# A two-layer trunk on one core: memory input, root columns, chunk steps and the last sums placed differently

## Chip, core and metric

The kernel runs on one core of one Trainium2 chip. The metric is the device time of one execution in microseconds; the median of three runs of the kernel before is 1064.99 us (1062.97 to 1065.62).

## What is computed

With the depth given, one layer of the trunk is run on x of 1024 tokens by 1024 features. RMS norm of x; a combined projection gives queries and keys q, k (4 heads of 96), values v (4 heads of 192), an output gate o, an input and a forget gate for each head, and queries for the memory. q and k pass a causal convolution of four taps and a SiLU. The mLSTM runs over chunks of 128 tokens with a running maximum:

```
s   = (q k^T) * w                      # w = exp(log weights - running maximum), causal
num = s v + a * (q C);  den = sum(s) + a * (q n)
h   = num / max(|den|, exp(-m))
C   = decay * C + (k*u)^T v ;  n = decay * n + sum(k*u)
```

Beside it, four heads attend to 256 memory vectors, whose keys and values are a projection of the RMS norm of mem. Both results, side by side, go through the output projection and are added to x. Then come RMS norm, a squared-ReLU MLP of width 4096, another addition, and a last RMS norm. All is float32.

## The kernel before

Tokens are worked on in two halves h of 512, with features on the 128 partitions. Each float32 product is made of three products of rounded parts (`mm3`, lines 110 to 112): high by high, high by low, low by high. So each weight tile goes through `load_w`: a load on SP's queue into one of 4 raw buffers, a rounding copy on ACT (L91) and a subtraction on POOL (L103) into one of 5 buffers. Activations are split likewise by `split` and `split_scaled` (L119 on ACT, L120 on DVE).

`run(dense, side, every)` weaves two generators: after every `every`-th step of the dense products it traces one step of the side work, and one function out of `later` (the convolutions of a group of blocks, appended when its products are done). With `finish` the rest of the side work is traced behind the dense one. What is traced sets priorities: a scheduler orders each engine's queue by a simulated timeline, taking what is ready and traced first, and places buffers of a ring as they come free. `tc.issue_after(i)` puts what a block traces on i's engine behind i; `tc.keep_in_program_order` does so among the instructions given to it. On the chip each engine and each DMA queue then takes its list in order.

The stages that the change touches, in order:

- `project_qk(0)`: 8 steps over the feature blocks k, with 6 product banks of PSUM; x is loaded through the ring `xr` of two buffers, split, squared. In step k = 6 the root over features is made (`rms`, L133 on, and `rms_cols`, L183, which moves the roots into columns by four small copies on DVE, L188). Behind it six scalings (L285), and in `later` six convolutions (L243 to L256).
- `project_v(0)`: 16 steps in two halves of 8, 4 banks each.
- `memory_load` reads mem in four loads through the ring `xr`; each is split into two blocks of `xm` and squared into `accm`. `xm` is the second buffer of the ring `qk`, whose first is written by L285. `memory_zeros` fills parts of the key and value matrices.
- `project_qmem(0)`, `memory_kv`: queries, keys and values of the memory; `rms` and `rms_cols` of accm stand behind the first key product of the second block. The root columns are read by the scaling of the values (L438). Beside them runs `gates(0)`, whose scan over columns (L471 on DVE) feeds a transposition on PE (gp, L476).
- `project_qk(1)`, then `project_v(1)`, 16 steps each, with the four chunks of the first half beside them: each `mlstm_chunk` has two yields, scores and keys (a), sums and state (b), and what follows the second yield, the output (c), runs on into the next chunk's a: nine pieces. In b, PE writes two heads' state sums into each of two banks (c, L548); DVE reads a head's sum (L552) before PE writes the other head's into the same bank.
- `last_chunk`: the last eighth of the second MLP product, output blocks b, first half 0 (512 tokens), then half 1 in two ranges of 256 (tok1, tok2). Every output block is added into x (L1241, or L1329 for the last two), squared on ACT, and the squares are added up on DVE (L1247, put off by `lag` until `flush`). `root_first` adds them over the partitions by products with ones (ssq_o, L159), and makes a root; `root_last` ends it (L172 to L176); `write` scales and stores.

Of the kernel before, what the change touches and what calls it, by code (L numbers as in the profile page):

```python
# [14 lines left out]
P = 128  # L15
# [3 lines left out]
HT = 512  # L19
# [16 lines left out]
def trunk_kernel(ctx, tc, a, out):  # L36
# [174 lines left out]
    def seq(*gens):  # L211
        for g in gens:
            yield from g


    att = ExitStack()
    mem = att.enter_context(tc.tile_pool(name="mem", bufs=1))
# [124 lines left out]
                    f()  # L342
            yield

    def query_weight(h, b, u):
        return load_w(a["w_qm"][b, u], 512, f"qm{h}{b}{u}")

    def query_ahead():

        st["qm_w", 0, 0, 0] = query_weight(0, 0, 0)  # L350
        yield

    def project_qmem(h):
        qm = mem.tile([P, 2, 2, HT], F32R, tag="qm", name=f"qm{h}")
        st["qm", h] = qm
        for b in range(2):
            p = ps(f"qm{h}{b}")
            for u in range(2):
                w = st.pop(("qm_w", h, b, u), None) or query_weight(h, b, u)
                for kk in range(4):  # L360
                    k = 4 * u + kk
                    c = slice(kk * P, (kk + 1) * P)
                    mm3(p, w[:, 0, c], w[:, 1, c], xa[:, 0, k], xa[:, 1, k], k == 0, k == KB - 1)
                if u == 0:
                    yield
            t = at.tile([P, HT], F32, tag="cacc", name=f"qmt{h}{b}", bufs=2)
            V.tensor_tensor(t, p, st["rbc", h], ALU.mult)
            split(qm[:, b, 0], qm[:, b, 1], t)
            yield
# [29 lines left out]
    def memory_kv():  # L399
        xm, acc = st["xm"]  # L400
        pk = []
        for b in range(2):
            p = ps(f"mk{b}")
            pk.append(p)
            for u in range(2):
                w = load_w(a["w_mk"][b, u], 512, f"mk{b}{u}")
                for kk in range(4):
                    k = 4 * u + kk
                    cc = slice(kk * P, (kk + 1) * P)
                    mm3(p[:, :NMEM], w[:, 0, cc], w[:, 1, cc], xm[:, k, 0], xm[:, k, 1], k == 0, k == KB - 1)  # L410
                if (b, u) == (1, 0):
                    parts = wpool.tile([P, 2, 512], F32R, tag="w", name="sums_m", bufs=5)
                    rbc, c = rms(acc, NMEM, "m", [parts[:, i] for i in range(2)])
                    rk = rms_cols(c, NMEM, "m")
                yield
        for b, p in enumerate(pk):
            t = at.tile([P, HT], F32, tag="cacc", name=f"mkt{b}", bufs=2)
            V.tensor_tensor(t[:, :NMEM], p[:, :NMEM], rbc[:, :NMEM], ALU.mult)
            for e in range(2):
                rows = slice(64 * e, 64 * e + 64)  # L420
                own = slice(NMEM * e, NMEM * e + NMEM)
                A.activation(kbd[rows, b, 0, own], t[rows, :NMEM], AF.Copy)
                V.tensor_tensor(kbd[rows, b, 1, own], t[rows, :NMEM], kbd[rows, b, 0, own], ALU.subtract)
        pv = [ps(f"mv{t}") for t in range(2)]
        for u in range(4):
            w = load_w(a["w_mv"][u], 512, f"mv{u}")
# [6 lines left out]
                        k == 0, k == KB - 1)  # L433
            if u < 3:
                yield
        for t in range(2):
            s = at.tile([P, HT], F32, tag="cacc", name=f"mvt{t}", bufs=2)
            V.tensor_scalar(s[:, :NMEM], pv[t][:, :NMEM], rk[:, t:t + 1], None, ALU.mult)  # L438
            s = s[:, :NMEM].rearrange("p (b e d) -> p b e d", b=2, e=2)
            for b in range(2):  # L440
                split(vmem[:, t, 0, b, 0::2], vmem[:, t, 1, b, 0::2], s[:, b])
# [236 lines left out]

    chunks = lambda h: seq(*(mlstm_chunk(h, t) for t in range(TPH)))

    run(project_qk(0), seq(wait(3), memory_zeros()))
    nc.sync.dma_start(gbias, a["gbias"].partition_broadcast(P))
    nc.sync.dma_start(whn, a["whn"].partition_broadcast(P))
    run(project_v(0), seq(memory_load(), wait(4), query_ahead()))
    run(seq(project_qmem(0), memory_kv()), seq(wait(3), gates(0)))
    run(project_o(0), tiles(0))
    run(seq(project_qk(1), project_v(1)), chunks(0), every=2)
    rest = seq(gates(1), tiles(1), chunks(1))
    run(seq(project_qmem(1), project_o(1, lambda k: transpose_y(0, k))), rest, finish=False)
    run(project_out(0, lambda k: transpose_y(1, k)), rest)  # L690
# [527 lines left out]
    def last_chunk():  # L1218
# [90 lines left out]
        tok2 = slice(HQ, HT)  # L1309
        acc2 = cm.tile([P, HT], F32, tag="acc", name="oacc2")  # L1310
        late = []
        for b in range(0, KB - 2, 2):
            p = ps(f"f2{b}2")
            for e in range(2):
                products(1, b + e, tok2, p, e * HQ)
            if b == 4:
                part = root_first([(ones, acc1[:, :HQ])], HQ, "o1")
            add(x1[1][:, b:b + 2, tok2], p.rearrange("p (e t) -> p e t", e=2), acc2, b == 0, f"2{b}")
            scale(1, [b, b + 1], tok2)
            if b == 0:  # L1320
                keep(V.tensor_tensor(acc1[:, :HQ], acc1[:, :HQ], acc1[:, HQ:], ALU.add))
        r1 = root_last(part, HQ, "o1")
        write(1, 0, tok1, r1, G)
        flush()
        for b in (KB - 2, KB - 1):
            p = ps(f"f2{b}2")
            products(1, b, tok2, p, 0)
            x = x1[1][:, b, tok2]
            keep(V.tensor_tensor(x, x, p[:, :HQ], ALU.add))  # L1329
            late.append(fp.tile([P, HT], F32, tag="sum", name=f"sq_o2{b}", bufs=3)[:, :HQ])  # L1330
            A.activation(late[-1], x, AF.Square)
        write(1, 2, tok1, r1, V)
        part = root_first([(ones, s) for s in [acc2[:, :HQ], acc2[:, HQ:], *late]], HQ, "o2")
        scale(1, [KB - 2, KB - 1], tok2)
# [79 lines left out]
```

## Time and profile before

| | |
|---|---|
| median of three runs | 1064.99 us (1062.97 to 1065.62) |
| profiled execution | 1062.4 us, of which the span of the trace is 1060.7 |
| PE busy | 1035.6 us, 98% of the span |
| DVE, POOL, ACT busy | 696.7 us (66%), 592.7 (56%), 545.5 (51%) |
| mean granted clock of PE | 0.993 |

The span runs from the first to the last instruction of one execution. Shares of busy time are averages over stages with different limits. PE is the matrix engine (PEld its weight loads), DVE the vector engine, ACT the scalar engine, POOL the general one, SP the engine whose queue issues the loads and stores. A releaser is inferred from semaphores.

### The profile page before, as it was taken

To read this page: it belongs to the slowest core of one execution; us is meant where nothing else is said; L and a number is where in the kernel's file an instruction comes from. 1 tells how busy PE (TensorE), PEld (TensorE's weight loads), DVE (VectorE), ACT (ScalarE), POOL (GpSimd) and SP (SyncE) were. 2 spreads that over 40 slices of the span, in tenths; PEclk is the share of its full clock that TensorE was granted. 3 is DMA by queue.
4 is the path that set the end of the run, shared out by engine and by line. 5 is a ranking of instruction groups with operands and counts; after the bars stand their busy time and mean duration, and the time that the engine had idled before them with its cause. 6 is when DMAs were issued, how large, how long until landed. Compare 5 with 4: busy or idle time off the path is not lost.

```text
span 1060.7 us, 14584 instructions
## 1 busy us (share of the span) xinstructions
PE 1035.6 (98%) x5018; PEld 887.1 (84%) x5018; DVE 696.7 (66%) x1122; ACT 545.5 (51%) x1050; POOL 592.7 (56%) x448
## 2 busy tenths in 40 slices
PE   9989999999999999999999999999999999999996
PEld 7988998899998888877888888887778888888885
DVE  6596885952766457996534433434899888878557
ACT  7464773344754354465665565555454433443273
POOL 6755435554424475004755566565568787776455
PEclk9999999999999999999999999999999999999999
DMA  7443333232324466326555453437775545544124
GB/s 223 115 126 109 115 122 87 69 93 89 99 60 120 151 190 196 100 65 215 198 186 184 155 189 134 172 120 239 258 212 174 158 142 167 152 137 139 54 78 158
DMA packets 81802, 152.46 MB, mean 144 GB/s; under 512 B 8096, under 2 KB 26560, under 8 KB 80192
## 3 DMA queue, kind: packets, MB, share of 16 engines
q1 hardware_dynamic: 81584, 151.51, 45.5%
q8 instruction: 39, 0.64, 0.3%
q14 instruction: 35, 0.29, 0.1%
q10 hardware_dynamic: 144, 0.03, 0.0%
HBM read 114.52 MB, written 36.19 MB: 142 GB/s over the span
## 4 chain that ended last, share of the span: by engine, by line
PE 73%; DVE 8%; DMA 6%; issue 5%; POOL 5%; ACT 3%; SPq 0%; DVEq 0%; POOLq 0%; ACTq 0%
PE fX L110 5%; PE fX L112 5%; PE fX L111 5%; DMA hr<-hd 4%; PE gX L112 3%; PE gX L111 3%; PE gX L110 3%; PE wo L110 3%; PE wo L112 3%; PE wo L111 3%; PE fZ L111 2%; PE fZ L110 2%; PE fZ L112 2%; PE o L110 2%; PE o L111 2%
## 5 line engine op out<-in xcount | busy, mean ns | idle before, releaser
L116 DVE TENSOR_TENSOR hb<-hr,hb 128x1024 fp32r<-128x1024 f32 x53 | 88.5, 1670 | 9.1 <-ACT hb L115 8.9
L1142 DVE TENSOR_TENSOR xo<-xo,gX 128x512 f32<-128x512 f32 x112 | 74.3, 682 | 26.9 <-PE gX L112 22.8
L111 PE MATMUL gX<-hb,w_b 128*128 128x512 f32 x224 | 87.3, 390 | 1.6 <-DVE hb L116 1.6
L110 PE MATMUL gX<-hb,w_b 128*128 128x512 f32 x224 | 86.4, 391 | 0.5 <-ACT hb L115 0.4
L112 PE MATMUL gX<-hb,w_b 128*128 128x512 f32 x224 | 85.5, 391 | 1.0 <-POOL w_b L797 1.0
L91 ACT ACTIVATE w_b<-S_b 128x512 fp32r<-128x512 f32 x56 | 34.9, 628 | 75.4 <-PE gX L112 33.5
L115 ACT ACTIVATE hb<-hr 128x1024 fp32r<-128x1024 f32 x53 | 55.8, 1053 | 32.4 <-DMA hr<-hd 32.0
L103 POOL TENSOR_TENSOR w_wo<-r_wo,w_wo 128x512 fp32r<-128x512 f32 x32 | 45.4, 1425 | 48.4 <-ACT w_wo L91 47.0
L797 POOL TENSOR_TENSOR w_b<-r_b,w_b 128x512 fp32r<-128x512 f32 x42 | 68.5, 1644 | 5.9 <-ACT w_b L91 5.9
L748 POOL TENSOR_TENSOR S_b<-r_b,r_b 128x512 f32<-128x512 f32 x28 | 44.9, 1605 | 32.7 <-DVE w_b L797 27.1
L797 POOL TENSOR_TENSOR w_a<-r_a,w_a 128x512 fp32r<-128x512 f32 x30 | 39.4, 1312 | 38.3 <-ACT w_a L88 37.5
L103 POOL TENSOR_TENSOR w_v<-r_v,w_v 128x388 fp32r<-128x388 f32 x32 | 39.5, 1245 | 31.9 <-ACT w_v L91 31.8
L103 POOL TENSOR_TENSOR w_o<-r_o,w_o 128x384 fp32r<-128x384 f32 x32 | 33.5, 1054 | 41.2 <-ACT w_o L91 41.2
L103 POOL TENSOR_TENSOR w_qk<-r_qk,w_qk 128x384 fp32r<-128x384 f32 x32 | 38.5, 1218 | 26.8 <-ACT w_qk L91 26.8
L110 PE MATMUL fX<-xa,w_a 128*128 128x512 f32 x128 | 50.1, 391 | 1.5 <-ACT hq L1004 1.2
L111 PEld LDWEIGHTS gX<-hb,w_b 128*128 128x128 f32 x224 | 42.1, 188 | 10.8 <-DVE hb L116 2.2
L110 PE MATMUL wo<-xa,w_wo 128*128 128x512 f32 x128 | 51.0, 400 | 0.0
L112 PEld LDWEIGHTS gX<-hb,w_b 128*128 128x128 f32 x224 | 42.1, 188 | 10.5 <-POOL w_b L797 1.8
L110 PEld LDWEIGHTS gX<-hb,w_b 128*128 128x128 f32 x224 | 41.9, 188 | 10.6 <-DVE xo L1142 1.0
L111 PE MATMUL wo<-xa,w_wo 128*128 128x512 f32 x128 | 50.1, 391 | 0.0
L112 PE MATMUL wo<-xa,w_wo 128*128 128x512 f32 x128 | 50.0, 390 | 0.0
L111 PE MATMUL fX<-xa,w_a 128*128 128x512 f32 x128 | 49.9, 389 | 0.0
(396 smaller groups left out, 3450.2 us busy)
## 6 DMA issues: line engine op xcount, KB each, us to landing
hr<-hd SPq DMA_DIRECT2D x53, 512.0 KB, 3.7
r_b<-w_ff SPq DMA_DIRECT2D x56, 256.0 KB, 3.0
hd<-hq SPq DMA_DIRECT2D x54, 256.0 KB, 2.0
hd<-hq SPq DMA_DIRECT2D x12, 1024.0 KB, 4.1
r_a<-w_ff SPq DMA_DIRECT2D x36, 256.0 KB, 2.7
r_wo<-w_out SPq DMA_DIRECT2D x32, 256.0 KB, 2.7
r_a<-w_ff SPq DMA_DIRECT2D x13, 512.0 KB, 4.6
r_v<-w_v SPq DMA_DIRECT2D x32, 194.0 KB, 2.4
```

Of the source, the lines that this page charges most:

```text
L91: st["first_part"] = A.activation(dst, src, AF.Copy).ins
L103: i = engine.tensor_tensor(w[:, 1, :n], raw[:, :n], w[:, 0, :n], ALU.subtract)
L110: keep(T.matmul(out, lhsT=lh, rhs=rh, start=start, stop=False, skip_group_check=goes_on))
L111: keep(T.matmul(out, lhsT=lh, rhs=rl, start=False, stop=False, skip_group_check=goes_on))
L112: keep(T.matmul(out, lhsT=ll, rhs=rh, start=False, stop=stop, skip_group_check=goes_on))
L115: A.activation(hi, src, AF.Copy)
L116: V.tensor_tensor(lo, src, hi, ALU.subtract)
L748: i = (on or (V if both is not None and sums_on_v and key != "S4" else G)).tensor_tensor(t, x, y, op)
L797: low = engine.tensor_tensor(w[:, 1], src, w[:, 0], ALU.subtract)
L1142: V.tensor_tensor(x, x, banks[e], ALU.add)
```

## The change

It does five things. `memory_load` is traced from the sixth step of `project_qk(0)` on, in turns with `memory_zeros` (a new helper `turns`), and what is left of both behind that projection; before, it ran from the first step of `project_v(0)`, and `memory_zeros` from the fourth step of `project_qk(0)`. The first query weight of the memory, which was loaded and split four steps after the memory input (`query_ahead`), is loaded in its own stage. `rms_cols` of the memory stands behind the values' products, and `issue_after` the last subtraction of the keys. The chunks of the first half take a step at every third step of `project_qk(1)`, and what is left at every second of `project_v(1)`. In the last range, the sum over partitions of the range before stands between the two products of b = 4, the squares of b = 4 are no longer added to those before but given to the last sum as two terms of their own, and the put-off addition of b = 2 follows b = 4's addition into x.

```diff
+    def turns(*gens):
+        gens = list(gens)
+        while gens:
+            for g in list(gens):
+                if next(g, gens) is gens:
+                    gens.remove(g)
+                else:
+                    yield
...
-    def query_ahead():
-
-        st["qm_w", 0, 0, 0] = query_weight(0, 0, 0)
-        yield
...
-                w = st.pop(("qm_w", h, b, u), None) or query_weight(h, b, u)
+                w = load_w(a["w_qm"][b, u], 512, f"qm{h}{b}{u}")
...
-                    rbc, c = rms(acc, NMEM, "m", [parts[:, i] for i in range(2)])
-                    rk = rms_cols(c, NMEM, "m")
+                    rbc, cols = rms(acc, NMEM, "m", [parts[:, i] for i in range(2)])
...
-                V.tensor_tensor(kbd[rows, b, 1, own], t[rows, :NMEM], kbd[rows, b, 0, own], ALU.subtract)
+                keys_made = V.tensor_tensor(kbd[rows, b, 1, own], t[rows, :NMEM], kbd[rows, b, 0, own],
+                                            ALU.subtract).ins
...
+        with tc.issue_after(keys_made):
+            rk = rms_cols(cols, NMEM, "m")
...
-    run(project_qk(0), seq(wait(3), memory_zeros()))
+    run(project_qk(0), seq(wait(5), turns(memory_load(), memory_zeros())))
...
-    run(project_v(0), seq(memory_load(), wait(4), query_ahead()))
+    run(project_v(0))
...
-    run(seq(project_qk(1), project_v(1)), chunks(0), every=2)
+    steps = chunks(0)
+    run(project_qk(1), steps, every=3, finish=False)
+    run(project_v(1), steps, every=2)
...
+        def add_last(x, p, nm):
+            keep(V.tensor_tensor(x, x, p, ALU.add))
+            sq = fp.tile([P, HT], F32, tag="sum", name=f"sq_o2{nm}", bufs=3)
+            flat = sq[:, :HQ] if len(x.shape) == 2 else sq.rearrange("p (e t) -> p e t", e=2)
+            A.activation(flat, x, AF.Square)
+            late.extend([sq[:, :HQ]] if len(x.shape) == 2 else [sq[:, :HQ], sq[:, HQ:]])
+
         for b in range(0, KB - 2, 2):
             p = ps(f"f2{b}2")
-            for e in range(2):
-                products(1, b + e, tok2, p, e * HQ)
+            products(1, b, tok2, p, 0)
             if b == 4:
                 part = root_first([(ones, acc1[:, :HQ])], HQ, "o1")
-            add(x1[1][:, b:b + 2, tok2], p.rearrange("p (e t) -> p e t", e=2), acc2, b == 0, f"2{b}")
+            products(1, b + 1, tok2, p, HQ)
+            x, halves = x1[1][:, b:b + 2, tok2], p.rearrange("p (e t) -> p e t", e=2)
+            if b < 4:
+                add(x, halves, acc2, b == 0, f"2{b}")
+            else:
+                add_last(x, halves, b)
+                flush()
...
-        flush()
         for b in (KB - 2, KB - 1):
...
-            x = x1[1][:, b, tok2]
-            keep(V.tensor_tensor(x, x, p[:, :HQ], ALU.add))
-            late.append(fp.tile([P, HT], F32, tag="sum", name=f"sq_o2{b}", bufs=3)[:, :HQ])
-            A.activation(late[-1], x, AF.Square)
+            add_last(x1[1][:, b, tok2], p[:, :HQ], b)
```

## Rows read from the trace of the kernel before

**Rows 1.** Waits of PE: line waited for, us in total, times, longest.
```profile
PE v L111 <- POOL w_v L103: 2.5, 2, 1.7
PE c L548 <- DVE C L552: 1.9, 1, 1.9
...
PE gp L476 <- DVE gaT L471: 1.7, 1, 1.7
PE gX L111 <- DVE hb L116: 1.6, 1, 1.6
...
PE v L110 <- ACT w_v L91: 1.1, 1, 1.1
```
**Rows 2.** Windows: length, each engine's busy us (instructions), PEclk, DMA share, GB/s.
```profile
40.00:60.00 20.00, 20.00 (x115) 20.00 (x114) 19.50 (x33) 10.64 (x23) 10.19 (x8) 1.00 0.39 104
...
76.00:80.00 4.00, 4.00 (x14) 3.65 (x13) 2.39 (x6) 3.90 (x8) 3.41 (x3) 0.57 0.73 194
103.00:107.00 4.00, 4.00 (x18) 4.00 (x19) 3.50 (x10) 2.95 (x8) 0.88 (x1) 0.57 0.56 157
206.00:210.00 4.00, 3.99 (x16) 3.92 (x17) 4.00 (x9) 1.75 (x3) 2.92 (x3) 0.58 0.01 2
...
735.00:741.00 6.00, 4.43 (x20) 3.26 (x19) 5.09 (x4) 4.24 (x7) 5.96 (x5) 1.00 0.57 206
```
**Rows 3.** Timeline of PE at the end: start, us, instruction, idle before and releaser.
```profile
1050.29 1.10 PE L159 MATMUL ssq_o<-oacc,ones 128*128 128x256 f32 x4 [1.85 <-DVE oacc L1247]
1051.23 1.03 PE L159 MATMUL ssq_o<-sq_o,ones 128*128 128x256 f32 x4
```
**Rows 4.** Tile xm: count, ns min/median/max, first and last start, form.
```profile
L120 DVE SCALAR_TENSOR_TENSOR xm<-xm,small,xm x8: 473/476/477, 44.9 to 71.3; 128x256 fp32r<-128x256 f32 x8
```
**Rows 5.** Tile accm, the same columns.
```profile
L129 DVE TENSOR_TENSOR accm<-accm,sq_m x3: 677/678/1777, 64.3 to 75.7; 128x512 f32<-128x512 f32 x3
L125 ACT ACTIVATE accm<-xm x1: 617/617/617, 25.6 to 25.6; 128x512 f32<-128x512 f32 x1
```
**Rows 6.** Timeline of ACT late in project_v(0).
```profile
63.52 0.62 ACT L128 ACTIVATE sq_m<-xm 128x512 f32<-128x512 f32 x1
64.04 0.62 ACT L91 ACTIVATE w_qm<-r_qm 128x512 fp32r<-128x512 f32 x1
...
65.70 0.51 ACT L91 ACTIVATE w_v<-r_v 128x388 fp32r<-128x388 f32 x1
...
72.04 0.61 ACT L128 ACTIVATE sq_m<-xm 128x512 f32<-128x512 f32 x1
72.56 0.51 ACT L91 ACTIVATE w_v<-r_v 128x388 fp32r<-128x388 f32 x1
```
**Rows 7.** Timeline of DVE at the end of project_qk(0).
```profile
34.97 0.72 DVE L144 STREAM_TRANSPOSE rt_x<-ssq_x 128x512 f32<-128x512 f32 x1 [9.56 <-PE ssq_x L142]
```
**Rows 8.** Timeline of DVE, memory stage and project_qk(1): root columns, scan.
```profile
98.76 3.49 DVE L188 COPY rk_m<-rc_m 32x2 f32<-32x2 f32 x4
102.28 0.41 DVE L471 TENSOR_TENSOR_SCAN gaT<-gaT 16x128 f32<-16x128 f32 x1
...
181.31 0.64 DVE L188 COPY rk_x<-rc_x 32x4 f32<-32x4 f32 x4
```
**Rows 9.** Timeline of PE in project_qk(1): half of the state sums.
```profile
199.28 0.82 PE L548 MATMUL c<-v,uk 128*96 128x193 f32 x4
```
**Rows 10.** Timeline of DVE in project_qk(1): the first read of them.
```profile
204.27 0.41 DVE L552 SCALAR_TENSOR_TENSOR C<-C,gdec,c 96x193 f32<-96x193 f32 x1
```
**Rows 11.** Timeline of DVE at the end.
```profile
1045.61 0.45 DVE L161 STREAM_TRANSPOSE rt_o<-ssq_o 128x256 f32<-128x256 f32 x1 [1.27 <-PE ssq_o L159]
...
1049.49 0.65 DVE L1247 TENSOR_TENSOR oacc<-oacc,sq_o 128x512 f32<-128x512 f32 x1
1050.06 0.74 DVE L1329 TENSOR_TENSOR xo<-xo,f 128x256 f32<-128x256 f32 x2
```
**Rows 12.** Timeline of ACT at the end.
```profile
1050.51 0.75 ACT L1331 ACTIVATE sq_o<-xo 128x256 f32<-128x256 f32 x2 [0.89 <-DVE xo L1329]
```

More of the change, by code (lines that the diff above doesn't have):

```diff
@@ L343, in project_o @@
             yield
-    def query_weight(h, b, u):
-        return load_w(a["w_qm"][b, u], 512, f"qm{h}{b}{u}")
-    def query_ahead():
-        st["qm_w", 0, 0, 0] = query_weight(0, 0, 0)
-        yield
     def project_qmem(h):
```

## The prediction

> **What bounds the kernel now.** Read the waits of TensorE first, longest at the top [rows 1]. One engine, PE, is nearly always busy, so the time is the matmuls plus the few gaps in them, and the question for each edit is which gap it can close. Three places carry almost all of it, two of them in one wait each. Place A is project_v(0): three waits on converted w_v weights (2.5 in two, 1.1 in one). Place B is the memory stage: 1.7 us for the scan of the gate columns (gp <- gaT). Place C is the first mLSTM half beside project_qk(1): 1.9 us, c <- C. Then come the stretches [rows 2]: the columns to read are PE busy and PEclk. Behind each of A, B and C there are 4 us in which PE is busy throughout, but at a mean granted clock of 0.57 or 0.58, that is partly at 1.2 instead of 2.4 GHz; 4 x 0.43 = 1.7 us are lost in each. So a gap costs more than its length: A 3.6 + 1.7 = 5.3, B 1.7 + 1.7 = 3.4, C 1.9 + 1.7 = 3.6. The fourth place is the tail, where PE is out of products at 1050.29 - 1.85 = 1048.44 [rows 3] and what follows is a chain over DVE, ACT, PE and DMA. All other waits of PE are shorter.
>
> Trace against rule: the gap of 1.6 us on gX [rows 1] was followed by no slow stretch, its window stands at 1.00 [rows 2], while 1.7 us at B was. The Trainium skill, "TensorE: Matmul & The Clock Gate", section "What's actually happening", says that the stretch over which the gate judges runs freely and doesn't start with the kernel; by it the same gap may cost the clock in one execution and not in the next. By that the 1.7 us that go with the gaps of A and of B below are gained in some executions only, and a gain of 10.6 us could shrink to 7.2.
>
> **Part 1, memory input into project_qk(0); the query weight no longer ahead (place A).** Moved are 4 loads on SP's queue, 8 scalings on ACT, 8 on DVE (476 ns each, 3.8 us), 4 squares on ACT, 3 additions on DVE (0.68 + 0.68 + 1.78 = 3.1 us) [rows 4, 5]; that is 6.9 us of DVE. The four zero steps go between them and later. Nothing is added; the one query weight (load, copy, subtraction) goes back to its own stage.
> Why A waits is read on ACT, which takes its work in order [rows 6]: the copy of a w_v weight at 65.70 stands behind a memory square (63.52) and the query weight's copy (64.04), each 0.52 us from its start to the next; the copy at 72.56 stands behind a square at 72.04. Taking them away brings the first copy forward by 1.0 us, more than half of the waits' mean (3.6 / 3 = 1.2), and the second by 0.5 plus whatever DVE gains, for the convolution's activations on ACT wait for DVE. On SP the w_v loads stop queuing behind the memory loads, on POOL behind the query weight's subtraction. Bounds: if the work finds DVE's idle 9.6 us before 34.97 [rows 7], all of A goes (5.3). If it stays where DVE is busy for 19.50 of 20 us [rows 2], only ACT's queue is shortened: 1.0 + 0.5 to be gained. The other end is a loss and is the third rival. I take 5.3: the first scalings ran at 44.9 [rows 4], early in that stretch, and the waits of A come at the end of the stage, when 3 of 4 memory steps would be long done. Its cover is that nothing needs the memory input before memory_kv; with that cover gone the mk products would wait instead.
> The page "SBUF — State Buffer" of the Trainium skill, section "Who interferes with whom", speaks against this part: a DVE operation with two SBUF inputs and a POOL operation that reads SBUF exclude each other. In the trace the last of the three additions took 1.78 instead of 0.68 us [rows 5]. By the rule the eight scalings, brought beside the w_qk and w_v subtractions of POOL, could each be stretched likewise by 1.1 us, 8.8 us in all, which is another way into the third rival; by the row of the eight, at 473 to 477 ns [rows 4], they cost 3.8.
>
> **Part 2, root columns behind the keys (place B).** Four copies on DVE, 3.49 us from 98.76 [rows 8], stand ahead of the scan at 102.28, for which PE waits. They now stand behind the last key subtraction. The scan can start at about 98.8, 3.5 us earlier, which is more than the 1.7 us wait: the wait and its slow stretch go, 3.4. What is late next is the keys, and they too come earlier. Behind the copies on DVE are now only the two scalings of the memory values, whose result is first used two tiles later in project_o(0); at worst they are as late as today. The price of the copies is 3.49 at most and 0.64 at least, which is what four such copies took at 181.31 [rows 8]. Bounds of the part: 0, if the key operations slip ahead of the scan, to 3.4; I take 3.4, for the scan's input is there first.
>
> **Part 3, chunk steps spread wider (place C).** Nothing is added. In project_qk(1) a step now comes after every third k instead of every second, and the last four of nine fall into project_v(1). In C PE had written one half of the state sums at 199.28; DVE read them only at 204.27 [rows 9, 10], since the convolutions of the first three blocks stood in its queue, and the second half shares the bank. With the new spacing there is less chunk work before the convolutions, so the lag of DVE should shrink; but step 3 (of 0 to 8) now falls behind product step 11, where step 5 fell, just behind the same convolutions, and the steps of chunks 2 and 3 run beside the convolutions of the second group and with four product banks open instead of three. Bounds: +3.6 (C goes), -3.6 (C stays or moves, and a second like it comes in project_v(1)). The nearest row is C's own, so neither end: I take +1.0.
>
> **Part 4, the tail.** The sum for the second range is now between the two blocks of b = 4, so DVE's transposition (1045.61) comes earlier, and the addition of squares at 1049.49 goes: 0.57 us to the next start [rows 11]. The diff has one such addition less in the loop, not three; in its place stand two more terms in the last sum. That sum took 8 instructions from 1050.29 to 1052.26, 0.246 each [rows 3]; now there are 12, 2.95 us. The last two additions into x (1050.06) can't both come before the products end, at 1048.44: they move forward by at most 1.6, and the last square with them, from 1051.26 [rows 12] to 1049.6. The first ten instructions need older terms and can start at 1048.44; so the sum ends at 1048.44 + 2.95 = 1051.4, 0.9 earlier. Bounds: 1.0 later (twelve from the old start) to 2.1 earlier (only the last two, 0.5, behind the last square). I take 0.9. What follows, root, scaling and output, is unchanged.
>
> **Sum.** 5.3 + 3.4 + 1.0 + 0.9 = 10.6 us. It is made against the profiled execution, 1062.4 us (span 1060.7); that lies 2.6 under the median of the runs, 1064.99, which is what I subtract from: 1054.4 us.
>
> **The rivals.**
> First, A stays in the main: the memory scalings can't use the idle stretch. For it: the first load had landed when ACT squared it at 25.6, yet DVE first scaled at 44.9, after 9.6 idle us [rows 4, 5, 7]; something other than data held them, as the first write to the other buffer of their ring. Then 1.5 + 3.4 + 1.0 + 0.9 = 6.8 us, 1058.2. Against it: ACT's queue is shorter in any case.
> Second, DVE becomes the bound in project_v(1): C stays or moves and a second such gap comes. 5.3 + 3.4 + 0.9 - 3.6 = 6.0 us, 1059.0. For it: DVE's lag of 5 us at C. With the first rival too, 2.2 us: 1062.8, no change.
> Third, slower: the 6.9 us of memory work on DVE, now ahead in the order, push the convolutions of project_qk(0) back by as much; ACT waits in order for them, and w_v copies stand behind. A's wait grows from 3.6 to 10.5 us and takes a second slow stretch, 1.7. Against B's 3.4 and the tail's 0.9 that is 6.9 + 1.7 - 4.3 = 4.3 us more, 1069.3. It decides the sign once the push is over 4.3 us, or 2.6 with the second slow stretch. For it: DVE's 19.50 of 20 us; against: most of that work already ran in the same stretch.
> Fourth, the planner that orders each queue places the moved steps where they were: B and the tail alone, 4.3 us, 1060.7.
>
> **Chances.** Forecast 0.46; first 0.16; second 0.15; first and second together 0.08; third 0.09; fourth 0.06. About 0.3% (3.2 us) is what a measurement tells from no change. Faster than 1061.8: the forecast, first and fourth wholly, the second nearly, less some for unequal parts: 0.73. Within: 0.17. Slower: 0.10. The range: the low end is all four parts at their best (5.3 + 3.4 + 3.6 + 2.1 = 14.4, 1050.6) less 0.8 for the spread of the runs; the high end takes in the two first rivals and their sum: 1049.8 to 1063.5.
>
> **What would show it.** Right: no wait of PE on w_v in project_v(0) and a granted clock of 1.00 throughout it; the memory scalings done by 50 us; the scan directly behind the memory root's transposition; gp without a wait; the last sum with 12 instructions, begun at the end of the products. Part 3 is right if c <- C is short in both projections. Wrong: a wait on w_v that stays or grows, ACT's activations of the convolution idling for DVE, or new waits in project_v(1) at 200 to 235 us.

## The result and the profile after

The changed kernel takes 1053.64 us (median of 4 runs, 1053.31 to 1054.95), the kernel before in the same comparison 1065.3 us (4 runs): ratio 0.9898, 95% interval 0.9877 to 0.9919. In a second comparison, with 6 runs, the ratio was 0.9905 (0.9882 to 0.9927). So the change gains 10 to 11 us, 1% of the time. The prediction was 1054.4.

The profiled execution after took 1053.31 us, its span 1051.6: 9.1 less than the profiled one before. The shares of busy time in it (us, share of the span, instructions):

```profile
PE 1031.4 (98%) x5022; PEld 883.3 (84%) x5022; DVE 696.0 (66%) x1121; ACT 545.1 (52%) x1050; POOL 590.8 (56%) x448
```

The waits of PE in it (us in total, times, longest), which answer to [rows 1]:

```profile
PE k L535 <- DVE wt L530: 1.7, 1, 1.7
PE ct L611 <- DVE pr L601: 1.6, 3, 0.8
PE gX L110 <- ACT hb L115: 1.5, 1, 1.5
PE v L110 <- DVE qk L295: 1.4, 1, 1.4
...
PE v L111 <- POOL w_v L103: 0.6, 2, 0.4
```

All the long waits of [rows 1] in the first 210 us are gone: on w_v (0.6 is left of 3.6), on the scan, on C. Three new ones stand in their places: v <- qk in A, ct <- pr behind B, k <- wt behind C. The windows (length, busy us of PE, PEld, DVE, ACT, POOL with instructions, PEclk, DMA share, GB/s) answer to [rows 2]:

```profile
40.00:60.00 20.00, 18.24 (x102) 17.60 (x101) 18.50 (x32) 10.27 (x20) 10.65 (x9) 1.00 0.36 96
76.00:80.00 4.00, 4.00 (x20) 3.30 (x19) 2.06 (x6) 3.32 (x8) 4.00 (x4) 1.00 0.56 148
95.00:99.00 4.00, 4.00 (x32) 3.84 (x31) 3.97 (x8) 2.60 (x7) 4.00 (x4) 1.00 0.22 63
195.00:199.00 4.00, 3.72 (x22) 3.57 (x23) 4.00 (x11) 1.28 (x4) 1.59 (x3) 1.00 0.36 101
```

Read PEclk: no stretch at the lower clock before the last 20 us of the span, although two gaps of 1.4 and 1.7 us are left. That is this execution; others of the same work had some, and the experiments come back to it.

The 9.1 us by stage, from the start of the same matmuls in both traces: the first memory key starts 3.4 earlier (89.77 to 86.33), the first memory scores 6.8 (107.83 to 101.06). The last v product ends 6.2 earlier: behind the scores ct <- pr takes 1.6 back, so that 1.0 is left for C's stage, by difference. From there to the end of the products, mostly MLP, which the change leaves alone but for its last range, it was 1.9 shorter; and from the end of the products to the end of the last sum it is 2.60 instead of 3.82.

### The profile page after: what moved, and what is told of

It is laid out like the page before. It is cut to its first block, busy times and chain, and to the rows that moved or that the text cites. A ratio compares the mean times of both kernels' runs of the same rounds, so it can differ in the third digit from the quotient of the medians.

```text
span 1051.6 us, 14594 instructions
## 1 busy us (share of the span) xinstructions
PE 1031.4 (98%) x5022; PEld 883.3 (84%) x5022; DVE 696.0 (66%) x1121; ACT 545.1 (52%) x1050; POOL 590.8 (56%) x448
## 4 chain that ended last, share of the span: by engine, by line
PE 73%; DVE 7%; DMA 6%; issue 6%; POOL 4%; ACT 3%; SPq 0%; DVEq 0%; POOLq 0%; ACTq 0%
PE fX L112 5%; PE fX L110 5%; PE fX L111 5%; PE gX L112 4%; PE gX L110 4%; PE gX L111 3%; DMA hr<-hd 3%; PE wo L110 3%; PE wo L112 3%; PE wo L111 3%; PE fZ L110 3%; PE fZ L112 2%; PE fZ L111 2%; PE gZ L112 2%; PE gZ L111 2%
## 5 line engine op out<-in xcount | busy, mean ns | idle before, releaser
L116 DVE TENSOR_TENSOR hb<-hr,hb 128x1024 fp32r<-128x1024 f32 x53 | 86.0, 1624 | 10.8 <-ACT hb L115 10.7
L103 POOL TENSOR_TENSOR w_v<-r_v,w_v 128x388 fp32r<-128x388 f32 x32 | 37.0, 1171 | 43.8 <-ACT w_v L91 43.6
L103 POOL TENSOR_TENSOR w_o<-r_o,w_o 128x384 fp32r<-128x384 f32 x32 | 35.8, 1129 | 39.4 <-ACT w_o L91 36.8
L110 PEld LDWEIGHTS gX<-hb,w_b 128*128 128x128 f32 x224 | 42.0, 188 | 11.7 <-ACT hb L115 1.9
L112 PEld LDWEIGHTS gX<-hb,w_b 128*128 128x128 f32 x224 | 42.1, 188 | 10.4 <-POOL w_b L803 1.8
L88 ACT ACTIVATE w_a<-S_a 128x512 fp32r<-128x512 f32 x63 | 39.2, 625 | 20.8 <-PE fZ L112 15.2
```

The lines of the kernel that those rows point to most:

```text
L88: i = A.activation(dst, src, AF.Copy)
L103: i = engine.tensor_tensor(w[:, 1, :n], raw[:, :n], w[:, 0, :n], ALU.subtract)
L110: keep(T.matmul(out, lhsT=lh, rhs=rh, start=start, stop=False, skip_group_check=goes_on))
L112: keep(T.matmul(out, lhsT=ll, rhs=rh, start=False, stop=stop, skip_group_check=goes_on))
L116: V.tensor_tensor(lo, src, hi, ALU.subtract)
```

## The experiments

The first four undo one part each, the others test what the four left open. "Before" was run beside all of them; ratios are to it. Where nothing is said, the edit stands against the changed kernel. By time alone the parts can't be told apart: the intervals of the runs without part 2, 3 or 4 overlap the changed kernel's two (0.9877 to 0.9927 together), and that of the run without part 1 (0.9926 to 0.9969) just touches them. What each part is worth is therefore read from the starts of the same matmuls, in one profile each.

**Part 1 undone.** The call order of before, with `query_ahead` back:

```diff
-    run(project_qk(0), seq(wait(5), turns(memory_load(), memory_zeros())))
-    run(project_v(0))
+    run(project_qk(0), seq(wait(3), memory_zeros()))
+    run(project_v(0), seq(memory_load(), wait(4), query_ahead()))
...
```

> The changed kernel with part 1 undone: memory input beside project_v(0) again, query weight ahead again. Theory (A was made by memory work in ACT's, SP's and POOL's queues): the waits on w_v late in project_v(0) come back, 3.6 us with a slow stretch of 1.7, and the new early wait (v <- qk, 1.4 us) goes: 3 to 4 us more than the changed kernel, about 1057. Rival (any new order of the queues shifts the gaps, the memory input has no part in it): within 1 us of the changed kernel, waits at other places.

1056.58 us, ratio 0.9947 (0.9926 to 0.9969). The waits of PE in this run: those on w_v are as before to a tenth, and v <- qk is gone.

```profile
PE v L111 <- POOL w_v L103: 2.5, 2, 1.7
...
PE v L110 <- ACT w_v L91: 1.1, 1, 1.1
```

But its window of 76 to 80 us, at 0.57 in [rows 2], is at full speed:

```profile
76.00:80.00 4.00, 4.00 (x21) 3.49 (x20) 2.38 (x7) 3.98 (x10) 3.70 (x4) 1.00 0.78 233
```

So the order that part 1 changes is what made the w_v weights late (the last experiment takes its halves apart), and the 1.7 us of clock that A was charged with come in one execution and not in another. The first memory key starts at 87.92 here, 1.6 us behind the changed kernel (86.33): 3.6 of waits on w_v against 2.0 that the changed kernel has in their place.

**Part 2 undone.** `rms_cols` back behind `rms`:

```diff
+                    rk = rms_cols(cols, NMEM, "m")
...
-        with tc.issue_after(keys_made):
-            rk = rms_cols(cols, NMEM, "m")
```

> The changed kernel with part 2 undone: root columns straight behind the memory root. Theory (the four copies hold up the scan): gp <- gaT comes back with 1.7 us and a slow stretch of 1.7; the new waits ct <- pr (1.6 us in three) go, for they come from scores that are due earlier: 2 us more, about 1055.6. Rival (the ct waits have another cause): they stay, 3.4 us more, about 1057.

1054.66 us, ratio 0.9928 (0.9904 to 0.9951). The waits of PE in this run: gp <- gaT is back at its old length.

```profile
PE gp L479 <- DVE gaT L474: 1.7, 1, 1.7
...
PE ct L610 <- DVE pr L600: 0.8, 2, 0.6
```

The window behind it has a slow stretch:

```profile
100.00:120.00 20.00, 19.20 (x102) 18.22 (x103) 16.41 (x44) 14.04 (x41) 8.32 (x10) 0.91 0.44 131
```

20 us at 0.91 are 1.8 us lost. From the first memory key to the first scores it takes 18.1 us here (87.60 to 105.68) and 14.7 in the changed kernel: 3.4. But ct <- pr is 0.8 instead of 1.6, neither gone, as the theory had it, nor the same, as the rival did: half of the new wait was hidden behind the old one.

**Part 3 undone.**

```diff
-    run(project_qk(1), steps, every=3, finish=False)
-    run(project_v(1), steps, every=2)
+    run(seq(project_qk(1), project_v(1)), chunks(0), every=2)
```

> The changed kernel with part 3 undone: chunk steps at every second step of both projections. Theory (spacing did not shorten PE's idle time, 2.2 us in both, but split it so that no slow stretch follows): the wait c <- C of 1.9 us comes back with its slow stretch, 1.5 to 2 us more, about 1055.3. Rival (the gap at C hung on where the queues stood before it, not on the spacing): no wait of C, within 0.7 us of the changed kernel.

1055.83 us (1051.62 to 1056.9), ratio 0.993 (0.9906 to 0.9953). In the timeline of PE in this run c <- C is back; k <- wt is gone:

```profile
198.67 1.27 PE L552 MATMUL c<-v,uk 128*96 128x193 f32 x4 [1.85 <-DVE C L556]
```

Its windows around that:

```profile
180.00:200.00 20.00, 18.14 (x95) 15.06 (x94) 19.06 (x42) 8.39 (x22) 11.32 (x8) 0.98 0.30 80
200.00:220.00 20.00, 20.00 (x108) 19.45 (x109) 19.93 (x50) 8.46 (x21) 9.87 (x10) 0.93 0.18 47
```

One gap of 1.85 us stands against one of 1.68: the idle time of PE is about the same with and without part 3, only at another place. What this profile loses there beyond the changed kernel is the slow stretch, 20 x 0.02 + 20 x 0.07 = 1.8 us. Its eight executions say the same: three at a mean granted clock of 0.996 or 0.997 took 1051.62 to 1053.4 us, no more than the changed kernel, five at 0.992 to 0.994 took 1055.79 to 1056.9. So no run shows that part 3 shortens PE's waits; what it gains is clock, in some executions.

**Part 4 undone.** The last range as before:

```diff
-            products(1, b, tok2, p, 0)
+            for e in range(2):
+                products(1, b + e, tok2, p, e * HQ)
             if b == 4:
                 part = root_first([(ones, acc1[:, :HQ])], HQ, "o1")
-            products(1, b + 1, tok2, p, HQ)
...
-            if b < 4:
-                add(x, halves, acc2, b == 0, f"2{b}")
-            else:
-                add_last(x, halves, b)
-                flush()
+            add(x1[1][:, b:b + 2, tok2], p.rearrange("p (e t) -> p e t", e=2), acc2, b == 0, f"2{b}")
...
+        flush()
         for b in (KB - 2, KB - 1):
...
```

> The changed kernel with part 4 undone: last ranges as before. Theory: only the tail differs, PE is idle 1.9 us ahead of the last sum, which has 8 instructions instead of 12; the end comes 1.0 to 1.3 us later, about 1054.8. Rival (POOL's contention, not the order, sets the chain): the same time within 0.4 us.

1054.96 us (1051.91 to 1057.3), ratio 0.9929 (0.9901 to 0.9957). The tail (end of the products to end of the last sum) is 3.81 us, as in the kernel before. The timeline of PE in this run:

```profile
1045.16 1.10 PE L159 MATMUL ssq_o<-oacc,ones 128*128 128x256 f32 x4 [1.84 <-DVE oacc L1253]
```

So part 4 is worth 1.2 us up to the end of the last sum, and the rival, by which the order has no part in it, falls. Far ahead of the tail, where this kernel is the changed one, the timeline of PE has the same gap v <- qk as in the profile after (1.38):

```profile
46.60 0.69 PE L110 MATMUL v<-w_v,xa 128*128 128x388 f32 x1 [1.37 <-DVE qk L295]
```

This time a slow stretch followed, as its window shows:

```profile
40.00:60.00 20.00, 17.61 (x91) 16.97 (x90) 17.67 (x31) 9.10 (x17) 12.04 (x8) 0.91 0.34 100
```

**The changed kernel again**, with no edit.

> The changed kernel itself, unchanged, a second profiled execution and a time beside the next three kernels. Theory (the gate's stretch runs freely, so that the same gap costs the clock in one execution and not in the next): the same gaps stand at the same places (v <- qk 1.4 in project_v(0), k <- wt 1.7 at the start of project_v(1), ct <- pr about 1.6 in three), each within 0.2 us, but the slow stretches behind them need not be the same as in the first profile, where there was none before 1040; with k gaps hit the span is 1051.6 + 1.7 k, give or take 0.5. Rival (what a gap does to the clock is fixed by the program): again no slow stretch before 1040, and a span within 0.5 of 1051.6. Time: 0.990 of the kernel before, between 0.988 and 0.992.

1053.22 us (1052.17 to 1056.3). v <- qk 1.4 and k <- wt 1.7 stand where they were, ct <- pr is 2.1, no stretch before the end is slow, span 1051.0. The run alone doesn't tell theory from rival; the profiles beside it do. k <- wt was 1.5 to 1.7 us in all twelve profiles of the changed kernel and of variants other than the one with part 3 undone. In four of them a slow stretch followed, in eight none. The timeline of PE in this run:

```profile
194.94 0.55 PE L535 MATMUL k<-ident,qk 96*128 96x96 f32 x4 [1.67 <-DVE wt L530]
```

Its window:

```profile
180.00:200.00 20.00, 18.14 (x98) 16.11 (x98) 17.78 (x42) 10.12 (x28) 7.99 (x9) 1.00 0.41 96
```

The run with the tiles later (below), whose engines went through the same lists, has the same gap in the timeline of PE:

```profile
195.49 0.55 PE L535 MATMUL k<-ident,qk 96*128 96x96 f32 x4 [1.67 <-DVE wt L530]
```

And its window:

```profile
180.00:200.00 20.00, 18.14 (x89) 16.03 (x88) 17.99 (x42) 9.83 (x27) 8.53 (x10) 0.92 0.39 103
```

PE was busy for 18.14 us in both windows and did 9 matmuls fewer in the second: 20 x 0.08 = 1.6 us lost to the clock behind the same gap (and 0.2 more in the next window, at 0.99). One program in many executions shows it without any edit: the kernel before, run 17 times beside the first four experiments, had mean granted clocks from 0.987 to 0.998, and took 1058.37 to 1067.85 us. So what a gap does to the clock isn't fixed by the program, and the rival falls. The Trainium skill, "TensorE: Matmul & The Clock Gate", section "What's actually happening", says that the stretch over which the gate judges runs freely; these runs agree with it.

**The root of x ahead.** The last block's memory scalings, and the additions of memory squares behind the first write, go behind the root's spreading on DVE:

```diff
+            with tc.issue_after(st["root_spread"]) if k == KB - 2 else nullcontext():
                 for i in range(2):
                     split_scaled(xm[:, k + i, 0], xm[:, k + i, 1], ...)
+            with tc.issue_after(st["root_spread"]) if k else nullcontext():
                 add_square(acc, raw, k == 0, f"m{k}")
...
```

> The changed kernel with the last block's memory scalings and all additions of memory squares but the first write put behind the spreading of x's root on DVE. Theory (the part-1 work, now ahead of x's root, delays the root on DVE and so the scalings that free the product banks): the root's reciprocal starts on DVE by 36.5 instead of 37.33, the spread ends before 40, the wait v <- qk (1.4 us) goes or falls under 0.3, the first product of the memory's queries starts 1.0 to 1.4 us earlier than in the changed kernel (75.43), and the time is 1 to 1.5 us (0.1%) shorter, more where the gap cost the clock. Rival (the power on POOL behind three w_v subtractions is what is late, whatever DVE does): the wait stays over 1.0 and the time is the same.

1052.71 us (1051.72 to 1055.33), ratio 0.99 (0.9877 to 0.9924). To see why the gap was there, read the timeline of DVE in the changed kernel (start, us, engine, line, operation, idle before and releaser), behind the transposition that [rows 7] shows of before:

```profile
36.18 1.23 DVE L129 TENSOR_TENSOR accm<-accm,sq_m 128x512 f32<-128x512 f32 x1 [0.68 <-ACT sq_m L128]
37.33 0.99 DVE L147 TENSOR_SCALAR rc_x<-rt_x 128x16 f32<-128x16 f32 x1
38.24 0.68 DVE L129 TENSOR_TENSOR accm<-accm,sq_m 128x512 f32<-128x512 f32 x1
40.95 0.88 DVE L120 SCALAR_TENSOR_TENSOR xm<-xm,small,xm 128x256 fp32r<-128x256 f32 x2 [2.03 <-ACT xm L119]
41.87 1.39 DVE L129 TENSOR_TENSOR accm<-accm,sq_m 128x512 f32<-128x512 f32 x1
43.18 0.70 DVE L150 STREAM_TRANSPOSE rr_x<-rc_x 128x512 f32<-128x512 f32 x1
```

The timeline of its ACT has what the scaling at 40.95 waited for:

```profile
40.41 0.91 ACT L119 ACTIVATE xm<-xm,small 128x256 fp32r<-128x256 f32 x2 [1.92 <-DMA xm<-memT]
```

And SP's queue in it:

```profile
28.47 8.75 SPq L96 DMA_DIRECT2D r_v<-w_v  x6
37.31 0.38 SPq L392 DMA_DIRECT2D xm<-memT  x1
```

The spreading stands on DVE behind the last memory block, whose load was issued at 37.31, behind six w_v loads. So x's root waits for a DMA of the memory. That is only the last 1.5 us of its delay. The root's power on POOL had ended at 38.90 in the kernel before, and ended at 41.70 in the changed one. The timeline of POOL before, and then after:

```profile
35.98 2.92 POOL L148 TENSOR_TENSOR rc_x<-rc_x,mhalf 128x16 f32<-128x16 f32 x1 [0.19 <-DVE rc_x L147]
```

```profile
34.86 3.43 POOL L103 TENSOR_TENSOR w_v<-r_v,w_v 128x388 fp32r<-128x388 f32 x3 [1.49 <-ACT w_v L91]
38.40 3.30 POOL L148 TENSOR_TENSOR rc_x<-rc_x,mhalf 128x16 f32<-128x16 f32 x1
```

The three w_v subtractions waited for their copies on ACT, which now stand behind memory scalings and zeros there: the first w_v copy starts at 34.27 us, before at 30.27. (DVE's operation at 37.33, which the power also needs, ended no earlier, at 38.32, behind an addition of memory squares.) The timeline of DVE with the root ahead:

```profile
36.26 0.37 DVE L147 TENSOR_SCALAR rc_x<-rt_x 128x16 f32<-128x16 f32 x1
41.46 0.71 DVE L150 STREAM_TRANSPOSE rr_x<-rc_x 128x512 f32<-128x512 f32 x1 [4.84 <-POOL rc_x L148]
```

Both sides have a point: v <- qk goes, as the theory had it, but the spread ends at 42.2 and not before 40, for POOL's power, behind three w_v subtractions, is now what ends last; the waits on w_v are 1.0 instead of 0.6. The queries start 0.6 us earlier (74.83), not the 1.0 to 1.4 of the theory, and the time can't be told from the changed kernel's.

**Steps at every third of project_v(1) too**:

```diff
-    run(project_v(1), steps, every=2)
+    run(project_v(1), steps, every=3)
```

> The changed kernel with the chunk steps after every third step of project_v(1) too, instead of every second. Theory (what is left at C is DVE's lag where chunk work and convolutions meet, so the gap moves with the spacing but isn't taken away): k <- wt (1.7) falls under 0.8 or moves, other waits on DVE in project_v(1) grow by as much, and the time is within 0.1% of the changed kernel. Rival (the wider spacing is itself what gains): the waits of PE between 150 and 240 us, 2.2 in all, fall by over 1.2 and the time by 1 to 3 us.

1055.68 us (1053.88 to 1058.06), ratio 0.9924 (0.9901 to 0.9946). k <- wt stayed at 1.7 to the hundredth (1.67), so neither side's number came true; no wait of PE is left in 200 to 220 us. In its profile the time was lost elsewhere, where the kernel is the changed one: v <- qk was 2.3 us, and the window of 40 to 60 us is at 0.91.

**Tiles a step later**:

```diff
-        yield from wait(3 - h)
+        yield from wait(2 if h else 4)
```

> The changed kernel with the transpositions of the first head group's probabilities in project_o(0) traced one step later. Theory (the chain behind the keys, columns and probabilities is now what PE waits for at the end of the memory stage, since B's scan is early): the three waits ct <- pr (1.6 in all, longest 0.8) fall under 0.4, the first products of project_o(0) run ahead, and the time is 1 to 1.6 us shorter. Rival (they only move to the next products that need them, co): ct <- pr goes, a wait of 1 us or more comes on co or o, and the time is the same within 0.5 us.

1055.5 us, ratio 0.9915 (0.9892 to 0.9938). ct <- pr is 1.6 in three, first ct at 112.33. But the edit did not do what it was meant to: PE, DVE, ACT and POOL each go through the same sequence of operations in this trace as in the changed kernel's, with 60 products o ahead of the first ct in both. The scheduler put the transpositions where they had been, so the run tests neither theory nor rival; it is another execution of the changed kernel's order.

**The shares first**, on top of the root ahead:

```diff
+        with tc.issue_after(st["shares", 0, 1]) if c < 3 else nullcontext():
             V.tensor_tensor(m, m, gt["mp"][...].broadcast_to([P, H, P]), ALU.max)
...
```

> The kernel of the run with the root ahead, and beside that the running-maximum additions of the first three chunks (m <- m, mp; 0.68 us each on DVE) put behind the memory probabilities of the first tile. Theory (ct <- pr, 1.5 us in three, is DVE's list: the second maximum over scores starts 6 us after PE made them since three such additions, the value splits and the gate columns stand ahead; two of the additions are between the first maximum and the second): the second maximum starts 1.4 to 2.0 us earlier against its scores, ct <- pr falls under 0.4, the first ct starts within 0.3 us of where PE is ready for it, and the time is 1 to 1.5 us shorter than with the root ahead alone (1052.7). Rival (the additions come back as a wait later, since chunk 0 in project_qk(1) needs them): ct <- pr goes, but a wait of PE of 1 us or more on wt or m comes in project_qk(1), before 175 us, and the time is the same.

1056.65 us, ratio 0.9942 (0.9924 to 0.996): worse. ct <- pr grew from 1.5 in three with the root ahead alone to 3.4 in six; another 1.8 us of this profile are a slow stretch behind k <- wt (windows of 180 to 220 us at 0.93 and 0.98). The timeline of ACT in this run gives the reason for the longest:

```profile
106.00 1.28 ACT L600 ACT_TABLE_LOAD   x1 [2.99 <-DVE guu L500]
107.30 0.47 ACT L600 ACTIVATE pr<-cs,cst 128x256 f32<-128x256 f32 x1
```

That of PE shows the wait:

```profile
109.17 0.70 PE L615 MATMUL ct<-ident,pr 128*128 128x128 f32 x4 [1.21 <-DVE pr L604]
```

The load of the exponential's table stands ahead of whichever exponential comes first here. In the changed kernel that was chunk 0's weights, with the load at 102.80, off the path; putting their input behind moved the load onto the path of the probabilities.

**The first exponential early**, against the run with the shares first:

```diff
-        with tc.issue_after(st["shares", 0, 1]) if c < 3 else nullcontext():
+        with tc.issue_after(st["shares", 0, 1]) if c in (1, 2) else nullcontext():
```

> The kernel of the run with the shares first, but the running-maximum addition of chunk 0 is left where it was; only those of chunks 1 and 2 stand behind the probabilities. Theory (that run's longer wait on ct, 1.2 us ahead of the first, was the load of ACT's exponential table, 1.28 us at 106.0, which chunk 0's weights had made at 102.8 off the path before): the table is loaded ahead of the probabilities again, the first ct waits under 0.3 us, ct <- pr is under 1.2 in all instead of 3.4, and ct begins within 34.8 us of the queries' start (35.6 there, 36.3 with the root ahead). Rival (the wait comes from DVE's and ACT's two passes between the maxima and the probabilities, whatever is ahead): ct <- pr stays over 1.8. Time, if the theory holds and no slow stretch comes: 1051 to 1053 us; each slow stretch adds 1.7.

1054.95 us (1053.22 to 1056.3), ratio 0.9921 (0.9896 to 0.9947). The timeline of ACT in this run:

```profile
100.42 1.28 ACT L522 ACT_TABLE_LOAD   x1
```

And that of PE:

```profile
107.98 0.70 PE L615 MATMUL ct<-ident,pr 128*128 128x128 f32 x4 [0.37 <-DVE pr L604]
```

The table is the answer for the first wait (1.21 to 0.37), and ct begins 34.74 us behind the queries. But ct <- pr is still 2.3 in five, as the rival had it: the passes between maxima and probabilities bind as well. From the queries' start to the first product with the memory's values (co) it takes 53.2 us here, 53.4 with the root ahead alone: nothing to gain on this way.

**Half of part 4**: the sum between the two products of b = 4, the squares of b = 4 added as before. Against the run with part 4 undone:

```diff
-            for e in range(2):
-                products(1, b + e, tok2, p, e * HQ)
+            products(1, b, tok2, p, 0)
             if b == 4:
                 part = root_first([(ones, acc1[:, :HQ])], HQ, "o1")
+            products(1, b + 1, tok2, p, HQ)
```

> The changed kernel with one half of part 4: the sum for the second range stays between the two products of b = 4, but the squares of b = 4 are added to those before on DVE again, with the put-off additions as in the kernel before. From the end of the products to the end of the last sum it was 3.82 us before and 2.60 with the whole of part 4. Theory (the dropped addition of squares is what gains, as the last sum's first products waited for it): 3.5 to 3.9 us, with a wait of PE on oacc of 1.4 us or more. Rival (the earlier sum for the second range frees DVE at the end, and that gains): 2.6 to 3.0 us, no wait over 0.7 on oacc. Time within 0.15% of the changed kernel either way.

The tail is 3.15 us, between theory and rival: 0.7 of the 1.2 come from the sum's place, 0.5 to 0.6 from the dropped addition and the place of the put-off one, which this run doesn't part. The timeline of PE in this run:

```profile
1049.15 1.10 PE L159 MATMUL ssq_o<-oacc,ones 128*128 128x256 f32 x4 [1.18 <-DVE oacc L1253]
1050.09 1.03 PE L159 MATMUL ssq_o<-sq_o,ones 128*128 128x256 f32 x4
```

And in the changed kernel, with no gap and four products more, where [rows 3] has a gap of 1.85:

```profile
1040.20 1.02 PE L159 MATMUL ssq_o<-oacc,ones 128*128 128x256 f32 x4
1041.07 1.89 PE L159 MATMUL ssq_o<-sq_o,ones 128*128 128x256 f32 x8
```

Its time (1056.34, ratio 0.9941, 0.992 to 0.9961) lies more above the changed kernel than the 0.55 us of tail explain. In its profile, the longest of its five executions (1061.29 us), v <- qk was 2.70 us with the window 40 to 60 us at 0.83, and the window 200 to 220 us is at 0.91 behind k <- wt, where it is the changed kernel too.

**Half of part 1**: the query weight ahead again, the memory input early.

```diff
-    run(project_v(0))
+    run(project_v(0), seq(wait(8), query_ahead()))
...
```

> The changed kernel with one half of part 1: the memory input stays in project_qk(0), but the first query weight of the memory is loaded and split ahead again, in the second half of project_v(0). Theory (the waits on w_v late in project_v(0) came from the memory squares and scalings in the lists of ACT and POOL; the query weight is 0.5 us of ACT and 1.3 us of POOL, less than the weights' lead): the waits on w_v in project_v(0) grow by less than 0.5 us over the changed kernel's (0.3 to 0.6 in all), the memory's queries start within 0.5 us of 75.4, and the time is the same within 0.1%. Rival (the query weight was what delayed the w_v weights): a wait of 1 us or more on w_v after 60 us comes back, and the queries start at 76.4 or later.

1058.13 us, ratio 0.9949 (0.9935 to 0.9964). The waits on w_v are 0.6 in all, in one wait. The timeline of PE in this run:

```profile
68.32 0.44 PE L111 MATMUL v<-w_v,xa 128*128 128x388 f32 x1 [0.56 <-POOL w_v L103]
```

The changed kernel has 0.26 there, the kernel before 3.6 in three: so not the query weight but the memory input had made w_v late, in the main. The queries start at 78.89 all the same, for v <- qk is 2.3 us with a slow stretch behind it (40 to 60 us at 0.91). That makes 3.5 us against the changed kernel's profile, and a slow stretch behind k <- wt (200 to 220 us at 0.91) 1.8 more, which is 5.3 of the 5.6 us between the two profiles. Why all six executions lie above the changed kernel's median stays open: the runs don't tell whether the edit made the long gap likelier.

## Why the prediction came out

**The bound.** Right: the gain came from gaps of PE and slow stretches behind them. Of the span's 9.1 us, PE's idle time gives 4.9 (25.1 to 20.2); the rest is PE's busy time (1035.6 to 1031.4), by estimate 5.1 less for the three slow stretches at 1.7 each and 0.8 more for four more products with ones. "Almost all" was too much for the three places: A, B and C held 7.2 of the 25.1 us of idle time.

**Part 1, predicted 5.3.** The step "the work finds DVE's idle 9.6 us" was right, and the first and fourth rivals fell with it: six of the eight scalings ran from 24.0 to 31.4 us, in that stretch, against [rows 4, 7]. The size was off: 3.4 by the first memory key. The term that was mis-sized is the cover: "its cover is that nothing needs the memory input before memory_kv". Nothing needs it, but the last block stands in DVE's list ahead of x's root, and so it became a wait of 1.4 us in the same stage: the third rival's mechanism, at a fifth of its price. How long it is hangs on when the last memory load lands. From its issue to ACT's first scaling it took 3.10 us in the profile after (37.31 to 40.41) and 3.78 in the run with half of part 4 (37.82 to 41.60). There DVE's scalings then met POOL's next w_v subtraction, and the two took 1.74 us instead of 0.88: gaps of 1.38 and 2.70. The timeline of DVE in that run, and then that of POOL:

```profile
42.14 1.74 DVE L120 SCALAR_TENSOR_TENSOR xm<-xm,small,xm 128x256 fp32r<-128x256 f32 x2 [2.70 <-ACT xm L119]
```

```profile
42.19 1.01 POOL L103 TENSOR_TENSOR w_v<-r_v,w_v 128x388 fp32r<-128x388 f32 x1
```

The two runs with a gap of 2.3 have 3.49 and 1.65 us for the same. (The run without part 2 has 1.75 us with a gap of 0.6: there PE came to it later.) By the start of the first memory key the gain of part 1 went from -0.6 (the run with half of part 4) to 4.6 and 5.7 us (the two runs on the shares, with the root ahead).

The row of tile xm after, against [rows 4] (count, ns min/median/max, first and last start):

```profile
L120 DVE SCALAR_TENSOR_TENSOR xm<-xm,small,xm x8: 472/485/650, 24.0 to 41.4; 128x256 fp32r<-128x256 f32 x8
```

That of accm, against [rows 5]:

```profile
L129 DVE TENSOR_TENSOR accm<-accm,sq_m x3: 678/1232/1389, 36.2 to 41.9; 128x512 f32<-128x512 f32 x3
```

In this profile the scalings weren't stretched by 1.1 us each: most of them fell outside POOL's subtractions, and the one of 650 ns ran beside one. Two of three additions, beside the w_v subtractions, were, by 0.55 and 0.71 us over 0.678. In five other profiles of kernels with this part the longest scaling took 1.24 to 1.35 us. So the rule of the Trainium skill, "SBUF — State Buffer", section "Who interferes with whom", shows here on the additions and on one scaling of some executions, not on all eight.

**Part 2, predicted 3.4.** Right: 3.4 between keys and scores by the run without it, 1.8 of it a slow stretch. In the timeline of DVE after, the scan stands directly behind the root's transposition, and the copies, which took 3.49 in [rows 8], take 0.68, near the lower bound:

```profile
94.97 0.42 DVE L150 STREAM_TRANSPOSE rr_m<-rc_m 128x256 f32<-128x256 f32 x1
95.33 0.85 DVE L475 TENSOR_TENSOR_SCAN gaT<-gaT 16x128 f32<-16x128 f32 x1
...
101.56 0.68 DVE L188 COPY rk_m<-rc_m 32x2 f32<-32x2 f32 x4
```

"What is late next is the keys" was wrong: late next are the memory probabilities, ct <- pr, 1.6 us, which the prediction didn't price. By the run without part 2, 0.8 of it is hidden when the scan is late.

**Part 3, predicted 1.0.** The stage gave 1.0, but by luck: the step "the lag of DVE should shrink" isn't borne out. c <- C [rows 1, 9, 10] turned into k <- wt, 1.7 instead of 1.9, as the second rival had it for the gap, without a second long one in project_v(1). What was gained is the slow stretch, which in four of twelve profiles is there all the same.

**Part 4, predicted 0.9.** Measured 1.2, of which 0.2 is lost again behind the sum. The addition of squares counted as 0.57 brought 0.55; PE has no gap ahead of the last sum. From the end of the products to the end of the sum it took 2.60 us instead of the estimated 2.95, and that is the difference: the twelve took 2.76, and the first started 0.16 ahead of the last product's end.

**The sum.** 3.4 + 3.4 - 1.6 + 1.0 + 1.0 = 7.2, and 1.9 from the stages between, 1.7 of it in the MLP, which the change doesn't touch: the stretch from the end of the output projection to the end of fX took 310.3 us before, 308.6 after, and 308.7 to 310.1 in the others. So it is partly luck that the time came out: part 1 too high by 1.9, ct not foreseen, and the scatter of the MLP made good for it. And the sum, made against one profile, was taken from the median of the runs, 2.6 above it: profile against profile the change gave 9.1 us of the 10.6 forecast, median against median 11.7 and 10.0 in the two comparisons. The changed kernel also keeps two gaps (v <- qk, k <- wt), each of which costs 1.6 to 1.8 us more in some executions: its runs spread from 1052.17 to 1056.3. No variant was shown to beat it.

## What to carry to other kernels

When work is moved into an idle stretch of an engine, look at the last piece of it: an engine that takes its list in order waits there for that piece's data, with all that stands behind. Before reading a run, see in its trace that the edit moved what it was meant to move: a scheduler may put it back. When a wait is removed, look which chain ended only a little earlier. And a gap of the matrix engine has two prices, its length and, in some executions, the slow stretch behind it: compare parts by the starts of the same matmuls, not by one time each.

## What the runs showed of the hardware

The same gap of 1.67 us was followed by full clock or by a loss of 1.6 to 1.8 us; gaps of 2.3 and 2.7 us in project_v(0) by a loss each of the three times. One program had mean granted clocks from 0.987 to 0.998. A scaling on DVE (128x256) took 0.47 to 0.49 us, and 1.34 beside a subtraction on POOL. Which exponential comes first decides where 1.28 us of table load fall.
